# Row normalization on one core: tiles of 16, 12, 12 and 11 rows in turn, with ScalarE summing part of the first tile

## The chip, the core and the metric

The kernel runs on one core of one Trainium2 chip. The metric is device time in microseconds, as a median over several executions. Every execution named here ran at a granted clock of 1.0 and is counted as fast, but for one: the kernel before with six rows reduced once more has an execution of 329.19 us that is classed as slow because it lies over 1.5% above the fastest of its kernel. It is left out of the comparisons. "Span" is the time from the first to the last instruction in the profile; the device time is 1.6 to 2.2 us longer than the span in all runs.

VectorE is written DVE in the profile, ScalarE is ACT, SyncE is SP. ACTq and SPq are the sequencers of ScalarE and SyncE; here their lines show where a DMA is issued.

## The reference

```python
x: float32 [32, 512, 1024]
sums = np.sum(np.abs(x), axis=-1, keepdims=True)
out  = x / (sums + 1e-8)
```

That is 16,384 rows of 1024 floats, or 128 rows of 4 KB on each of the 128 partitions: 67.1 MB read and 67.1 MB written.

## The kernel before

Each tile gives every partition R consecutive rows, so each partition's part of a load or store is one contiguous run of R x 4 KB. All loads are issued by SyncE, all stores by ScalarE. VectorE sums, and VectorE and ScalarE each multiply half of the rows.

```python
    R = 12
    BUFS = 4
    rows = [R] * (per_partition // R)          # ten tiles of 12
    if per_partition % R:
        rows.append(per_partition % R)         # and one of 8
    # ... cut: piece(), which slices x and out by tile ...
    sbuf = ctx.enter_context(tc.tile_pool(name="sbuf", bufs=BUFS))
    stats = ctx.enter_context(tc.tile_pool(name="stats", bufs=4))

    def normalize(x_tile, r0, k, kv):
        s = stats.tile([P, R], FP32)
        nc.vector.tensor_reduce(out=s[:, :k], in_=x_tile[:, r0 : r0 + k, :],
            axis=mybir.AxisListType.X, op=mybir.AluOpType.add,
            apply_absolute_value=True)
        nc.vector.tensor_scalar_add(out=s[:, :k], in0=s[:, :k], scalar1=EPS)
        inv = stats.tile([P, R], FP32)
        nc.vector.reciprocal(out=inv[:, :k], in_=s[:, :k])
        nc.vector.tensor_mul(...)              # rows 0 to kv-1, times inv
        for r in range(kv, k):                 # the other rows, on ScalarE
            nc.scalar.activation(...)          # Copy, scale=inv[:, r]

    with tc.manual_schedule():
        for i, k in enumerate(rows):
            x_tile = sbuf.tile([P, R, d], FP32)
            nc.sync.dma_start(out=x_tile[:, :k, :], in_=piece(x_flat, i))
            normalize(x_tile, 0, k, k // 2)
            nc.scalar.dma_start(out=piece(out_flat, i), in_=x_tile[:, :k, :])
```

With four buffers, loads 0 to 3 are issued at once. Load 4 has to wait until store 0 has landed, load 5 for store 1, and so on. Load 3 is therefore the last load that waits for nothing.

Of the kernel before, what the change touches and what calls it, by code (L numbers as in the profile page):

```python
# [1 line left out]

# [4 lines left out]

FP32 = mybir.dt.float32
EPS = 1e-8


@with_exitstack
def kernel(
    ctx: ExitStack,
    tc: tile.TileContext,
    x: bass.AP,
    out: bass.AP,
):
    nc = tc.nc
    P = nc.NUM_PARTITIONS  # L20

    x_flat = x.flatten_outer_dims()
    out_flat = out.flatten_outer_dims()
    n, d = x_flat.shape


    R = 12
    BUFS = 4
    per_partition = n // P
    assert n % P == 0  # L30
    rows = [R] * (per_partition // R)
    if per_partition % R:
        rows.append(per_partition % R)

    def piece(flat, i):
        a, k = P * sum(rows[:i]), rows[i]
        return flat[a : a + P * k, :].rearrange("(p r) d -> p r d", p=P)

    sbuf = ctx.enter_context(tc.tile_pool(name="sbuf", bufs=BUFS))
    stats = ctx.enter_context(tc.tile_pool(name="stats", bufs=4))  # L40

    def normalize(x_tile, r0, k, kv):

        s = stats.tile([P, R], FP32)
        nc.vector.tensor_reduce(  # L45
            out=s[:, :k],
            in_=x_tile[:, r0 : r0 + k, :],
            axis=mybir.AxisListType.X,
            op=mybir.AluOpType.add,
            apply_absolute_value=True,  # L50
        )
        nc.vector.tensor_scalar_add(out=s[:, :k], in0=s[:, :k], scalar1=EPS)  # L52
        inv = stats.tile([P, R], FP32)
        nc.vector.reciprocal(out=inv[:, :k], in_=s[:, :k])  # L54
        nc.vector.tensor_mul(  # L55
            out=x_tile[:, r0 : r0 + kv, :],
            in0=x_tile[:, r0 : r0 + kv, :],
            in1=inv[:, :kv].unsqueeze(2).to_broadcast([P, kv, d]),
        )
        for r in range(kv, k):  # L60
            row = x_tile[:, r0 + r, :]
            nc.scalar.activation(  # L62
                out=row,
                in_=row,
                func=mybir.ActivationFunctionType.Copy,
                scale=inv[:, r : r + 1],
            )

    with tc.manual_schedule():
        for i, k in enumerate(rows):  # L70
            x_tile = sbuf.tile([P, R, d], FP32)
            nc.sync.dma_start(out=x_tile[:, :k, :], in_=piece(x_flat, i))  # L72
            normalize(x_tile, 0, k, k // 2)
            nc.scalar.dma_start(out=piece(out_flat, i), in_=x_tile[:, :k, :])  # L74


# [1 line left out]
_INS = ['x']  # L78
_OUTS = [((32, 512, 1024), 'float32')]


# [23 lines left out]
```

## Time and profile before

| | before |
|---|---|
| device time, median of 3 | 317.64 us (317.47 to 317.89) |
| span | 315.8 us |
| DVE, ACT busy | 67%, 22% |
| bytes moved | 134.23 MB, 425 GB/s over the span |
| first store issued | 38.45 us |

The page of the profile, cut to the busy rows. Each digit is the busy share of one of 40 slices, in tenths:

```profile
span 315.8 us, 227 instructions
...
## 2 busy tenths in 40 slices
DVE  0069999998499079719944991797099449949300
ACT  0010804308007000700440070007003400701300
...
DMA  8999999999999999999999999999999999999996
```

The DMA row is at 9 but for the first slice and the last, while VectorE has holes. So the engines wait for DMA, and not DMA for them. The next view gives the same for stretches of time. Its columns are start:end, length, busy time and instruction count of DVE, ACT and POOL, granted clock, DMA share, and GB/s. A transfer counts where it starts, so a short stretch can read above or below its share.

```profile
core 0: us, DVE busy (x) ACT busy (x) POOL busy (x), PEclk, DMA share, GB/s
...
83.00:100.00 17.00, 16.63 (x4) 3.28 (x4) 0.00 (x0) 1.00 1.01 439
120.00:160.00 40.00, 30.72 (x8) 11.61 (x12) 0.00 (x0) 1.00 1.00 433
...
200.00:240.00 40.00, 30.88 (x5) 6.34 (x6) 0.00 (x0) 1.00 1.00 433
...
310.00:315.00 5.00, 0.00 (x0) 0.00 (x0) 0.00 (x0) 1.00 0.55 236
315.00:320.00 5.00, 0.00 (x0) 0.00 (x0) 0.00 (x0) 1.00 0.01 2
```

From 83 to 280 us the DMA share is 1.00 to 1.01, at 433 to 439 GB/s. The last row shows that next to nothing moves after 315 us.

The timeline of the first tile (start, length, engine, line, operation, shapes, and in brackets the idle time before it and what ended that):

```profile
18.35 12.95 DVE L45 TENSOR_REDUCE s<-x_tile 128x12 f32<-128x12288 f32 x1 [18.35 <-DMA x_tile<-in_x_dram]
18.40 1.28 ACT L62 ACT_TABLE_LOAD   x1 [18.40 <-DMA x_tile<-in_x_dram]
...
31.81 6.34 ACT L62 ACTIVATE x_tile<-x_tile,inv 128x1024 f32<-128x1024 f32 x6 [12.13 <-DVE inv L54]
31.81 6.56 DVE L55 TENSOR_TENSOR x_tile<-x_tile,inv 128x6144 f32<-128x6144 f32 x1
...
38.45 0.37 ACTq L74 DMA_DIRECT2D out_dram<-x_tile  x1
```

The first tile lands at 18.35 us, is summed for 12.95 us, is multiplied on both engines, and its store is issued at 38.45 us.

A finer reading comes from the trace's records of single DMA packets, which are not a view of the profile. A packet is one partition's run of a tile: 48 KB for 12 rows. A 48 KB packet takes 1.815 us and one of 32 KB takes 1.213 us.

### The profile page before, as it was taken

How to read it: one execution, taken by the hardware profiler on the slowest of the kernel's cores; microseconds unless marked ns; L12 is line 12 of the kernel's file. 1: busy time of each engine (PE TensorE's matmuls, PEld its weight loads, DVE VectorE, ACT ScalarE, POOL GpSimd, SP SyncE). 2: the span in 40 equal slices, each digit the busy share in tenths (PEclk: the TensorE clock that was granted, in tenths of full speed). 3: DMA queues.
4: the chain of work that ended last, by engine and by line, in shares of the span. 5: the costliest groups of instructions: out<-in, count | busy, mean ns of one | idle time of the engine just before them, and what ended most of it. 6: DMA issues, size and time to landing. Idle time of an engine off the chain costs nothing.

```text
span 315.8 us, 227 instructions
## 1 busy us (share of the span) xinstructions
DVE 212.4 (67%) x44; ACT 69.0 (22%) x65; POOL 0.2 (0%) x4
## 2 busy tenths in 40 slices
DVE  0069999998499079719944991797099449949300
ACT  0010804308007000700440070007003400701300
POOL 0000000000000000000000000000000000000000
DMA  8999999999999999999999999999999999999996
GB/s 311 467 417 411 467 367 442 405 454 430 417 448 430 423 461 423 436 442 417 442 442 411 449 436 411 448 436 423 448 430 436 442 413 450 421 448 417 448 403 278
DMA packets 3169, 134.23 MB, mean 425 GB/s; under 512 B 352, under 2 KB 352, under 8 KB 352
## 3 DMA queue, kind: packets, MB, share of 16 engines
q1 hardware_dynamic: 1584, 67.11, 49.8%
q10 hardware_dynamic: 1584, 67.11, 49.1%
q14 instruction: 1, 0.01, 0.0%
HBM read 67.11 MB, written 67.11 MB: 425 GB/s over the span
## 4 chain that ended last, share of the span: by engine, by line
DMA 55%; DVE 25%; another core or an unknown queue 9%; ACT 4%; issue 0%; SPq 0%; DVEq 0%; ACTq 0%
DMA x_tile<-in_x_dram 41%; DVE s L45 19%; DMA out_dram<-x_tile 14%; DVE x_tile L55 6%; ACT x_tile L62 4%; DVE inv L54 0%; DVE s L52 0%; SPq L72 0%; DVEq L54 0%; ACTq L74 0%
## 5 line engine op out<-in xcount | busy, mean ns | idle before, releaser
L45 DVE TENSOR_REDUCE s<-x_tile 128x12 f32<-128x12288 f32 (+1 forms) x11 | 138.2, 12564 | 81.1 <-DMA x_tile<-in_x_dram 81.1
L62 ACT ACTIVATE x_tile<-x_tile,inv 128x1024 f32<-128x1024 f32 x64 | 67.7, 1135 | 207.6 <-DVE inv L54 207.6
L55 DVE TENSOR_TENSOR x_tile<-x_tile,inv 128x6144 f32<-128x6144 f32 (+1 forms) x11 | 70.0, 6364 | 0.4
L62 ACT ACT_TABLE_LOAD x1 | 1.3, 1283 | 18.4 <-DMA x_tile<-in_x_dram 18.4
L54 DVE RECIPROCAL inv<-s 128x12 f32<-128x12 f32 (+1 forms) x11 | 2.5, 226 | 0.9
L52 DVE TENSOR_SCALAR s<-s 128x12 f32<-128x12 f32 (+1 forms) x11 | 1.9, 173 | 0.4
L89 POOL MEMSET const-bfloat16-1.0<- 128x1 bf16 x1 | 0.1, 101 | 0.0
L89 POOL MEMSET const-uint8-127<- 128x1 uint8 x1 | 0.1, 101 | 0.0
L89 POOL MEMSET const-float32-0.0<- 128x1 f32 x1 | 0.1, 98 | 0.2 <-issue 0.2
L89 POOL MEMSET const-float32-1.0<- 128x1 f32 x1 | 0.1, 98 | 0.0
## 6 DMA issues: line engine op xcount, KB each, us to landing
x_tile<-in_x_dram SPq DMA_DIRECT2D x10, 6144.0 KB, 38.5
out_dram<-x_tile ACTq DMA_DIRECT2D x10, 6144.0 KB, 53.5
x_tile<-in_x_dram SPq DMA_DIRECT2D x1, 4096.0 KB, 33.7
out_dram<-x_tile ACTq DMA_DIRECT2D x1, 4096.0 KB, 19.5
```

The costliest lines, as they stand in the source:

```text
L45: nc.vector.tensor_reduce(out=s[:, :k], in_=x_tile[:, r0 : r0 + k, :], axis=mybir.AxisListType.X, op=mybir.AluOpType.add, apply_absolute_v ...
L52: nc.vector.tensor_scalar_add(out=s[:, :k], in0=s[:, :k], scalar1=EPS)
L54: nc.vector.reciprocal(out=inv[:, :k], in_=s[:, :k])
L55: nc.vector.tensor_mul(out=x_tile[:, r0 : r0 + kv, :], in0=x_tile[:, r0 : r0 + kv, :], in1=inv[:, :kv].unsqueeze(2).to_broadcast([P, kv, d]),)
L62: nc.scalar.activation(out=row, in_=row, func=mybir.ActivationFunctionType.Copy, scale=inv[:, r : r + 1],)
L89: nc = _bacc.Bacc("TRN2", target_bir_lowering=False, num_devices=1)
```

## The change

The intent, as the diff reads: give each partition 51 rows of buffers in place of 48, use longer runs in ten tiles rather than eleven, and keep the first store from coming late behind the longer first tile by letting ScalarE sum six of its sixteen rows.

```diff
-    R = 12
-    BUFS = 4
+    R = 16
+    SLOTS = [R, 12, 12, 11]
     # ... cut: rows are taken from SLOTS in turn: 16, 12, 12, 11, 16, 12, 12, 11, 16, 10 ...
-    sbuf = ctx.enter_context(tc.tile_pool(name="sbuf", bufs=BUFS))
+    slots = [
+        ctx.enter_context(tc.tile_pool(name=f"slot{b}", bufs=1))
+        for b in range(len(SLOTS))
+    ]
     stats = ctx.enter_context(tc.tile_pool(name="stats", bufs=4))
+    psum = ctx.enter_context(tc.tile_pool(name="psum", bufs=1, space=bass.MemoryType.PSUM))
+    junk = psum.tile([P, d], FP32)
-    def normalize(x_tile, r0, k, kv):
+    def normalize(x_tile, k, ks, kv):
         nc.vector.tensor_reduce(
-            out=s[:, :k],
-            in_=x_tile[:, r0 : r0 + k, :],
+            out=s[:, :ks],
+            in_=x_tile[:, :ks, :],
             # ... cut ...
+        for r in range(ks, k):
+            nc.scalar.activation(
+                out=junk[:, :],
+                in_=x_tile[:, r, :],
+                func=mybir.ActivationFunctionType.Abs,
+                accum_out=s[:, r : r + 1],
+            )
     # ... cut ...
-            normalize(x_tile, 0, k, k // 2)
+            normalize(x_tile, k, k if i else k * 5 // 8, k // 2)
```

More of the change, by code (lines that the diff above doesn't have):

```diff
@@ L24 @@
     n, d = x_flat.shape
-    R = 12
-    BUFS = 4
-    per_partition = n // P
+    R = 16
+    SLOTS = [R, 12, 12, 11]
     assert n % P == 0
-    rows = [R] * (per_partition // R)
-    if per_partition % R:
-        rows.append(per_partition % R)
+    left = n // P
+    rows = []
+    while left:
+        rows.append(min(left, SLOTS[len(rows) % len(SLOTS)]))
+        left -= rows[-1]
     def piece(flat, i):
@@ L55, in normalize @@
         nc.vector.tensor_mul(
-            out=x_tile[:, r0 : r0 + kv, :],
-            in0=x_tile[:, r0 : r0 + kv, :],
+            out=x_tile[:, :kv, :],
+            in0=x_tile[:, :kv, :],
             in1=inv[:, :kv].unsqueeze(2).to_broadcast([P, kv, d]),
@@ L60, in normalize @@
         for r in range(kv, k):
-            row = x_tile[:, r0 + r, :]
+            row = x_tile[:, r, :]
             nc.scalar.activation(
@@ L70 @@
         for i, k in enumerate(rows):
-            x_tile = sbuf.tile([P, R, d], FP32)
+            x_tile = slots[i % len(SLOTS)].tile([P, SLOTS[i % len(SLOTS)], d], FP32)
             nc.sync.dma_start(out=x_tile[:, :k, :], in_=piece(x_flat, i))
-            normalize(x_tile, 0, k, k // 2)
+            normalize(x_tile, k, k if i else k * 5 // 8, k // 2)
             nc.scalar.dma_start(out=piece(out_flat, i), in_=x_tile[:, :k, :])
```

## The prediction

> **What bounds the kernel now.** The DMA engines, nearly from end to end. The page's DMA row reads 9 in 38 of 40 slices; the windows view gives a DMA share of 1.00 to 1.01 in each stretch from 83 to 280 us, at 433 to 439 GB/s. In the trace's DMA packets all 16 engines have a packet running for about 302 of the 315.8 us. A packet is one partition's 48 KB and takes 1.815 us: 27.1 GB/s an engine, 433 GB/s for sixteen. The Trainium skill, "DMA: Bandwidth & Descriptors", section "Where 436 GB/s comes from", puts the ceiling of the ports at 435.2 GB/s; this trace agrees, at 433. The bytes (134.2 MB) do not change and need about 310 us at that rate. What is left: 1.7 us before the first packet, about 1 us because each engine's first packet takes 2.3 to 3.4 us, about 1 us when the first stores join (one slow load packet per engine after 40 us), and the end (last packet 314.2, span 315.8, time 317.6).
>
> DVE is 67% busy, ACT 22%. DVE waits for loads (81.1 us, by the waits view), which costs nothing while DMA is full. The chain of waits holds compute steps (reduce 19%), but they run beside a full DMA.
>
> **What the change does.**
> - Tiles of 16, 12, 12, 11, 16, 12, 12, 11, 16, 10 rows in place of ten of 12 and one of 8; four buffers still, 51 rows in place of 48.
> - Packets of 64, 48, 44 and 40 KB. From 1.213 us for 32 KB and 1.815 for 48 KB a packet costs some 9 ns plus 0.1505 us a row, so 64 KB should take 2.42 us. Sixteen packets fewer per engine save about 0.15 us.
> - The first load lands later: four rows at 1.21 us, so about 23.2 us in place of 18.35. The first reduce takes ten rows, 10.8 us (12.95/12 a row), while ACT sums six: table load 1.28 us, then six at some 1.1 to 1.4 (estimate from the 1.135 us scale), at most 9.7 us, hidden under the reduce. The multiply of eight rows takes 8.75 us. First store issued near 43.3, in place of 38.45.
> - 16-row tiles later keep DVE 26 us, still under their DMA time of 39 us.
>
> **How much lies on the critical path.** Almost none. I worked the order of packets through with these durations (loads and stores alternating by packet, a load waiting for the store four tiles before). Loads run until about 90 us; store 0 lands near 80, so load 4 is queued before load 3 ends. At no later point are both queues empty. The narrowest place is the end: the last 16-row store is issued near 274 and its predecessor ends near 281; the 10-row store near 291, against 301. A later first store costs nothing: loads fill the time.
>
> **Predicted: 317.4 us, 316.6 to 318.8 in 8 of 10.** Faster by over 2%: 0.01; within 2%: 0.95; slower by over 2%: 0.04.
>
> **What would show it.** Full DMA share from 10 us to 310; 64 KB packets of 2.42 us; first store issued at 43 to 44; the Abs group done before the first reduce; the last load landing near 274; the last packet ending within 1 us of 314.
>
> **What would make it wrong.** A gap in DMA near 80 or 275 to 282 us, if a store is issued later than I reckon. Or 64 KB packets slower than in proportion: their rows start at a power-of-two pitch. The same page ("Latency and other measured facts") measured slower copies from a pitch of 512 KiB up; 64 KiB is well below, and the 8-row tile, at 32 KB, showed none (1.213 us).

## More of the kernel before

Placing each packet after the one that ended as it started sorts them into 16 lanes of 176 packets each, taken here as one lane for each DMA engine (the records do not name the engine). In a lane one packet follows the next without a gap.

Packets that took longer than their size asks for cost 2.19 us per engine in all: 0.96 in the first 5 us, when the first loads start, and 1.16 between 36 and 60 us, when the first store joins.

## The result, and the profile after

| | before | after |
|---|---|---|
| device time, median of 4 | 317.76 us (317.47 to 317.96) | 318.09 us (317.94 to 318.18) |
| ratio after/before | | 1.0011, 95% interval 0.9993 to 1.0028 |
| span | 315.8 us | 315.9 us |
| first store issued | 38.45 us | 42.66 us |
| slow packets, us per engine | 2.19 | 2.06 |
| last data packet ends | 314.2 us | 314.5 us |

A ratio is the mean time of one kernel's runs over that of the other's in the same rounds, so it is not quite the ratio of the medians. The interval includes 1: the two kernels can't be told apart.

The page after, cut to the same rows:

```profile
span 315.9 us, 228 instructions
...
## 2 busy tenths in 40 slices
DVE  0019999999449701999799079807950499999000
ACT  1017730803400800009108000700160002806000
...
DMA  9999999999999999999999999999999999999996
```

The DMA row is the same, while the VectorE row has other holes. The stretches of time, for the changed kernel:

```profile
83.00:100.00 17.00, 8.90 (x1) 0.00 (x0) 0.00 (x0) 1.00 0.99 429
120.00:160.00 40.00, 32.86 (x5) 8.43 (x8) 0.00 (x0) 1.00 0.99 427
...
200.00:240.00 40.00, 21.54 (x5) 9.90 (x10) 0.00 (x0) 1.00 1.00 431
...
310.00:315.00 5.00, 0.00 (x0) 0.00 (x0) 0.00 (x0) 1.00 0.47 205
315.00:320.00 5.00, 0.00 (x0) 0.00 (x0) 0.00 (x0) 1.00 0.01 2
```

The DMA share is 0.99 to 1.00 in the long stretches shown (1.01 in the one from 160 to 200 us), and again nearly nothing moves after 315 us. The first tile:

```profile
0.72 1.28 ACT L61 ACT_TABLE_LOAD   x1 [0.72 <-PEq L106]
...
22.45 10.82 DVE L53 TENSOR_REDUCE s<-x_tile 128x10 f32<-128x10240 f32 x1 [22.45 <-DMA x_tile<-in_x_dram]
22.45 1.03 ACT L61 ACTIVATE junk<-x_tile 128x1024 f32<-128x1024 f32 x1 [20.45 <-DMA x_tile<-in_x_dram]
23.42 0.18 ACT L61 ACTIVATION_READ_ACCUMULATOR junk<-x_tile 128x1 f32 x1
...
29.32 0.18 ACT L61 ACTIVATION_READ_ACCUMULATOR junk<-x_tile 128x1 f32 x1
...
33.88 8.69 DVE L70 TENSOR_TENSOR x_tile<-x_tile,inv 128x8192 f32<-128x8192 f32 x1
33.88 8.42 ACT L77 ACTIVATE x_tile<-x_tile,inv 128x1024 f32<-128x1024 f32 x8 [4.38 <-DVE inv L69]
...
42.66 0.37 ACTq L91 DMA_DIRECT2D out_dram<-x_tile  x1
```

The first tile lands four rows later, at 22.45 us. VectorE sums ten rows in 10.82 us. ScalarE's six sums run beside it and end at 29.5 us, 3.8 us before VectorE's reduce does. The first store is issued at 42.66 us, 4.2 us later than before, and the end of the kernel hardly moves.

Two things about ScalarE's part are seen only here. The groups of instructions (busy us and mean ns after the bar, then idle time):

```profile
L61 ACT ACTIVATE junk<-x_tile 128x1024 f32<-128x1024 f32 x6 | 6.2, 1028 | 20.6 <-DMA x_tile<-in_x_dram 20.4
...
L61 ACT ACT_TABLE_LOAD x1 | 1.3, 1283 | 0.7 <-PEq L106 0.7
L61 ACT ACTIVATION_READ_ACCUMULATOR junk<-x_tile 128x1 f32 x6 | 1.1, 185 | 0.0
```

Each sum is two instructions, the Abs of 1028 ns and a read of the accumulator of 185 ns, and they start 1.18 us apart. The table load of 1283 ns ran at 0.72 us, while ScalarE had nothing to do, and not after the landing as I had assumed. The Trainium skill, "ScalarE: Activation LUTs", section "What ACT_TABLE_LOAD costs", gives about 1283 ns for that load; this trace has the same.

### The profile page after: what moved, and what is told of

It is laid out like the page before. It is cut to its first block, busy times and chain, and to the rows that moved or that the text cites. A ratio compares the mean times of both kernels' runs of the same rounds, so it can differ in the third digit from the quotient of the medians.

```text
span 315.9 us, 228 instructions
## 1 busy us (share of the span) xinstructions
DVE 204.2 (65%) x40; ACT 76.8 (24%) x78; POOL 0.2 (0%) x4
## 4 chain that ended last, share of the span: by engine, by line
DMA 37%; another core or an unknown queue 29%; DVE 26%; SPq 0%; issue 0%; DVEq 0%; ACTq 0%
DMA x_tile<-in_x_dram 21%; DVE s L53 16%; DMA out_dram<-x_tile 16%; DVE x_tile L70 9%; SPq L87 0%; DVE inv L69 0%; DVE s L67 0%; DVEq L69 0%; DVEq L67 0%; ACTq L91 0%
## 5 line engine op out<-in xcount | busy, mean ns | idle before, releaser
L53 DVE TENSOR_REDUCE s<-x_tile 128x12 f32<-128x12288 f32 (+3 forms) x10 | 131.6, 13164 | 86.5 <-DMA x_tile<-in_x_dram 86.5
L77 ACT ACTIVATE x_tile<-x_tile,inv 128x1024 f32<-128x1024 f32 x65 | 68.6, 1135 | 194.0 <-DVE inv L69 194.0
L70 DVE TENSOR_TENSOR x_tile<-x_tile,inv 128x6144 f32<-128x6144 f32 (+2 forms) x10 | 68.8, 6878 | 0.3
L61 ACT ACTIVATE junk<-x_tile 128x1024 f32<-128x1024 f32 x6 | 6.2, 1028 | 20.6 <-DMA x_tile<-in_x_dram 20.4
L69 DVE RECIPROCAL inv<-s 128x12 f32<-128x12 f32 (+3 forms) x10 | 2.3, 234 | 0.8
L67 DVE TENSOR_SCALAR s<-s 128x12 f32<-128x12 f32 (+3 forms) x10 | 1.7, 174 | 0.4
L61 ACT ACT_TABLE_LOAD x1 | 1.3, 1283 | 0.7 <-PEq L106 0.7
L61 ACT ACTIVATION_READ_ACCUMULATOR junk<-x_tile 128x1 f32 x6 | 1.1, 185 | 0.0
## 6 DMA issues: line engine op xcount, KB each, us to landing
out_dram<-x_tile ACTq DMA_DIRECT2D x1, 5120.0 KB, 22.4
```

Of the source, the lines that this page charges most:

```text
L53: nc.vector.tensor_reduce(out=s[:, :ks], in_=x_tile[:, :ks, :], axis=mybir.AxisListType.X, op=mybir.AluOpType.add, apply_absolute_value=True,)
L61: nc.scalar.activation(out=junk[:, :], in_=x_tile[:, r, :], func=mybir.ActivationFunctionType.Abs, accum_out=s[:, r : r + 1],)
L70: nc.vector.tensor_mul(out=x_tile[:, :kv, :], in0=x_tile[:, :kv, :], in1=inv[:, :kv].unsqueeze(2).to_broadcast([P, kv, d]),)
L77: nc.scalar.activation(out=row, in_=row, func=mybir.ActivationFunctionType.Copy, scale=inv[:, r : r + 1],)
```

## The experiments

**Theory going in:** the 16 DMA engines are full, so the time is the start, plus the bytes at their rate, plus the end. When the first store comes does not matter as long as loads last. **Rival:** the two halves of the change cancel; the bigger tiles make the first store later and cost time, and ScalarE's sums win it back.

### Both halves alone, and no compute at all

**The changed kernel without ScalarE's sums.**

```diff
-            normalize(x_tile, k, k if i else k * 5 // 8, k // 2)
+            normalize(x_tile, k, k, k // 2)
```

> The changed kernel without ScalarE's sums in the first tile: the first reduce takes 17.2 us in place of 10.8, so the first store is issued near 49 us in place of 42.7. Theory (the 16 DMA engines are full from 4 us on, so the time is start + bytes at their rate + end, and the moment of the first store does not matter): 318.1 us, within 0.5 us of the changed kernel. Rival (the two halves of the change cancel: bigger tiles cost what the later first store loses, and ScalarE's sums win it back): some 6 us slower, near 324.

Measured: 324.55 us median of 6, ranging from 322.38 to 326.01, ratio to before 1.0214 (1.0177 to 1.0252): slower beyond the noise, though whether by over 2% is unclear. **My theory missed; the rival's number came in.** The timeline of its first tile shows that the edit did what was meant:

```profile
22.61 17.22 DVE L53 TENSOR_REDUCE s<-x_tile 128x16 f32<-128x16384 f32 x1 [22.61 <-DMA x_tile<-in_x_dram]
...
40.36 8.69 DVE L70 TENSOR_TENSOR x_tile<-x_tile,inv 128x8192 f32<-128x8192 f32 x1
...
49.13 0.38 ACTq L91 DMA_DIRECT2D out_dram<-x_tile  x1
```

Its page:

```profile
span 321.2 us, 216 instructions
...
DMA  9999999999997999999999999999999999999993
```

Still nearly all nines, so the 6 us are no gap that this row could show. Its last stretches:

```profile
310.00:315.00 5.00, 0.00 (x0) 0.00 (x0) 0.00 (x0) 1.00 0.89 385
315.00:320.00 5.00, 0.00 (x0) 0.00 (x0) 0.00 (x0) 1.00 0.30 131
```

In the kernel before, data after 315 us came to 2 GB/s over five microseconds. Here 131 GB/s still move there: some engines are late. The completion records say how many. The first engine to finish its last store reported at 314.1 us, close to the 313.2 us of before. Six engines were done by 314.6 us, and the other ten followed between 315.8 and 320.1 us; in before the last one reported at 314.7 us. Slow packets cost 5.31 us per engine on average, in place of 2.06 in the changed kernel. The records of three lanes, two of this run and one of the changed kernel (L is a load, S a store, then rows, start + length in us; * marks a packet slower than its size asks for):

```
no ScalarE sums, a lane:   L11:55.7+1.67 S16:57.4+3.06* L11:60.4+1.67 S16:62.1+3.31* L11:65.4+1.67 S16:67.1+3.54*
no ScalarE sums, another:  L11:57.3+1.67 S16:59.0+2.42 L11:61.4+2.19* S16:63.6+2.42 L11:66.0+2.16* S16:68.1+2.43
changed kernel, a lane:    L11:61.5+1.67 S16:63.2+2.42 L11:65.6+1.67 S16:67.3+2.42 L11:69.7+1.67 S16:71.3+2.42
```

Loads and stores alternate packet by packet, as the Trainium skill, "DMA: Bandwidth & Descriptors", section "Queues, rings and completion order", says of an engine with work from two queues. In the slow run the engines fell into two groups, one starting a store while the other loads, and packets in both are slow while store 0 goes out. Sixteen more slow ones, one per engine on average, come at 95 to 96 us, when load 4 joins the running stores (2.5 to 4.6 us in place of 2.42). In the changed kernel all 16 engines load and store in step.

**The kernel before with ScalarE's sums, and nothing else.**

```diff
+        for r in range(ks, k):
+            nc.scalar.activation(out=junk[:, :], in_=x_tile[:, r, :],
+                func=mybir.ActivationFunctionType.Abs, accum_out=s[:, r : r + 1])
-            normalize(x_tile, 0, k, k // 2)
+            normalize(x_tile, 0, k, k // 2, k if i else 7)
```

(The reduce takes the first `ks` rows, as in the change; junk is the same PSUM tile.)

> The kernel before with ScalarE summing five of the first tile's twelve rows and nothing else changed: the first reduce takes 7.6 us in place of 12.95, so the first store is issued near 33 us in place of 38.4. Theory: 317.8 us, within 0.5 us of before. Rival (halves cancel): some 5 us faster, near 312.5.

Measured: 317.72 us, ratio 1.0001 (0.9989 to 1.0013), with the first store issued at 33.28 us. Here my theory held and the rival missed by 5 us: an earlier first store gains nothing.

**The kernel before with no compute** (the line that calls `normalize` is taken out; a wrong result).

> The kernel before with all compute taken out, so that it only loads and stores (wrong result on purpose): a floor. First store issued near 18.5 us. Theory: DMA was full already, so 317 to 318 us, at most 1 us under before. Rival (compute is on the path, as the chain of waits with 25% DVE may suggest): clearly faster, 300 us or less if a quarter of the chain went.

Measured: 317.45 us, ratio 0.9993 (0.9981 to 1.0005). Its page:

```profile
span 315.4 us, 80 instructions
...
DMA  8999999999999999999999999999999999999996
```

This is a floor for this pattern of loads and stores, and both kernels already stand within 0.7 us of it. Compute that is only made quicker cannot win anything here. Yet the first experiment shows that compute can still lose.

### The slow packets when stores start

**The kernel before with the first load split over two queues.**

```diff
+            if i == 0:
+                h = k // 2
+                nc.sync.dma_start(out=x_tile[:, :h, :], in_=src[:, :h, :])
+                nc.scalar.dma_start(out=x_tile[:, h:k, :], in_=src[:, h:, :])
```

> The kernel before with the first load in two halves, rows 0 to 5 from SyncE's queue and rows 6 to 11 from ScalarE's. About 40 us from the start of before, one load packet per engine takes 2.6 to 3.2 us in place of 1.815, when the first stores join: 1.1 us per engine in all. Theory A (that is the price of the first use of the second queue): the slow packets near 40 us go, and the time falls by about 1 us, to 316.8. Theory B (it is the price of the first data going out of SBUF): the slow packets stay and the time is within 0.4 us of before.

Measured: 317.69 us, ratio 1.0002 (0.9990 to 1.0014). Between 36 and 60 us 22 packets are still slow, for 1.08 us per engine. So it is not the first use of the second queue that costs this; here it comes when the first stores join running loads. That it is the stores as such is not shown, and two later runs (first store at 66 and 84 us) speak against it: their first stores, with no load running, take at most 2.47 us in place of 2.42, and 32 slow packets, loads and stores, come instead when load 4 joins the stores, for 2.3 us per engine. Nothing is won.

### How late may the first store be?

**The changed kernel, with the first tile's 16 rows reduced twice, and three times** (`for _ in range(times)` around the first tile's reduce, times = 2 and 3; the result is the same).

> The changed kernel with the first tile's reduce over all 16 rows run twice on VectorE (the same result): first store issued near 66 us. The four buffers hold 51 rows, which loads alone fill by 64.4 us (at 1.213 us a row). Theory (only a gap in DMA costs): DMA idles for about 3.4 us from 64.4, so 321.5 us (320.5 to 322.5). Rival 1 (the first store's delay is passed on): about 23 us slower, 341. Rival 2 (later slack takes it all up): 318.1.

> The same with the reduce run three times: first store issued near 84 us. Theory: a DMA gap of about 20.6 us from 64.4, so 338.7 us (337 to 340.5), every further microsecond of delay now passed on one for one (17.2 more than the run with two reduces). Rival 1 (delay passed on from the first microsecond): near 359. Rival 2 (slack takes it up): 318.

Measured: 322.11 us (321.72 to 322.69) and 339.0 us (338.94 to 339.26), with the first store at 66.3 and 83.6 us. Both numbers came in. The last load that waits for nothing landed at 64.9 and 65.0 us, and from then until the store there is nothing to move. For the second, in stretches:

```profile
50.00:60.00 10.00, 9.97 (x2) 0.00 (x0) 0.00 (x0) 1.00 1.00 433
60.00:65.00 5.00, 5.00 (x1) 0.00 (x0) 0.00 (x0) 1.00 0.67 288
65.00:70.00 5.00, 5.00 (x1) 0.00 (x0) 0.00 (x0) 1.00 0.00 0
70.00:80.00 10.00, 9.90 (x4) 5.14 (x5) 0.00 (x0) 1.00 0.00 0
80.00:84.00 4.00, 4.00 (x2) 3.28 (x4) 0.00 (x0) 1.00 0.00 0
84.00:90.00 6.00, 6.00 (x1) 0.00 (x0) 0.00 (x0) 1.00 1.22 524
```

From 65 to 84 us DMA moves nothing. From that point every microsecond of delay is passed on. But 322.11 us, with a real gap of some 3 us and with these slow packets, is *less* than the 324.55 us of the run with its store at 49 us and no gap.

### Less buffer, smaller tiles

**The kernel before with BUFS = 3.**

> The kernel before with three buffers of 12 rows in place of four. If DMA need only be kept from running empty, 36 rows nearly suffice: worked through packet by packet, one gap of about 1 us near 304 us, at the end, when the last store is issued just after the one before has gone: 318.8 us (317.8 to 320). Rival (buffer capacity is what the time hangs on, so that 51 rows against 48 should have helped): several us slower, over 322.

Measured: 318.72 us (318.50 to 319.13), ratio 1.0040. The short gap is where it was reckoned:

```profile
302.00:304.00 2.00, 2.00 (x1) 2.00 (x3) 0.00 (x0) 1.00 0.91 393
304.00:306.00 2.00, 0.50 (x1) 0.28 (x1) 0.00 (x0) 1.00 0.61 262
306.00:308.00 2.00, 0.00 (x0) 0.00 (x0) 0.00 (x0) 1.00 1.16 492
```

The last store is issued at 304.58 us, just as its predecessor runs out. Losing a quarter of the buffers costs 1 us, by a gap that the kernel before does not have, so 51 rows in place of 48 had hardly anything to gain.

**The kernel before with R = 4 and BUFS = 12.**

> The kernel before with 4 rows a tile and 12 buffers, the same 48 rows in all. From the packets' durations (1.213, 1.815, 2.418 us for 32, 48, 64 KB) each packet costs about 9 ns besides its bytes; this kernel has 512 packets per engine in place of 176 and needs 3.0 us more by that: 320.8 us (320 to 322.5). Rival (smaller tiles start stores sooner and end sooner, so finer is better): under 316.

Measured: 318.39 us, ratio 1.0025 (1.0010 to 1.0040). It is slower, as expected, but by 0.7 us and not 3. A 16 KB packet does take 0.611 us, as the 9 ns a packet would have it. But the records of neighbouring packets overlap a little, here by 1.76 us per engine and in before by 0.50, and slow packets cost less here, 1.36 us per engine against 2.19. Taken off the 3.0 us, that leaves 3.0 - 1.26 - 0.83 = 0.9 us, near the 0.7 measured. So the 9 ns that I read off the durations overstate what a packet costs in time.

### Lateness, tile sizes, or something else?

The first experiment needed a new theory. Theory A: lateness of the first store costs about its own length. Theory B: it takes unequal packets (64 KB stores against 44 KB loads) and a chance split of the engines, or a load queue that has run dry.

**The changed kernel with ScalarE summing three rows** (13 in place of `k * 5 // 8`).

> The changed kernel with ScalarE summing three of the first sixteen rows in place of six: first reduce over 13 rows, first store issued near 46 us (42.7 in the changed kernel, 49.1 with no ScalarE sums, which came out 6 us slower). Theory A (a later first store costs about as much as it is late): near 321.5. Theory B (the run with no ScalarE sums was slow because its first store split the 16 DMA engines into two groups half a load-store cycle apart, and 64 KB stores against 44 KB loads then ran slow until that store had gone, and because the load queue ran dry near 85 us): here the store still joins while 48 KB loads run and lands near 84 us, before the last of load 3, so 318.1 us (317.5 to 319) unless the engines split again.

Measured: 318.9 us (318.46 to 319.72), ratio 1.0041. That is theory B's range, and no 3.4 us for 3.4 us of lateness.

**The changed kernel with no ScalarE sums and six rows reduced once more first.**

```diff
+        if again:
+            nc.vector.tensor_reduce(out=s[:, :again], in_=x_tile[:, :again, :], ...)
-            normalize(x_tile, k, k if i else k * 5 // 8, k // 2)
+            normalize(x_tile, k, k, k // 2, 0 if i else 6)
```

> The changed kernel with no ScalarE sums and six rows reduced once more first: first store issued near 55.6 us, while all engines load the 44 KB packets of tile 3. Theory A (lateness costs): near 330, or at least above 325. Theory B (gaps, the price of a queue starting again, and a chance split): loads run dry near 71 us while stores go on, so no gap, one more start of a queue of about 1 to 2 us: 319 to 320.5 us, faster than with the store at 49; above 322 only if the engines split here too.

Measured: 318.74 us median of 4 (317.56 to 321.6), ratio 1.0047 (0.9984 to 1.0111). The first store is 7 us *later* than in the run that took 324.55 us, and the time is 6 us shorter. Theory A falls. The median is just under theory B's range. Its price for a queue that starts again did not show: the loads ran dry at 75.4 us and began again at 85, with one slow packet. One of the four executions, not the profiled one, still took 321.6 us, near the loss of the slow run; in the profiled one 15 engines were done by 313.7 us and one at 316.0.

**The kernel before with six rows reduced once more first** (the same edit; all its packets are 48 KB, but for the last tile).

> The kernel before with six rows of the first tile reduced once more first: first store issued near 44.9 us in place of 38.4, the same lateness of 6.4 us that cost 6 us in the unequal tiles, here with loads and stores of one size, 48 KB. Theory A (lateness costs in any kernel): near 323. Theory B (it took unequal packets, or a dry load queue; here store 0 lands near 77 us and load 3 near 83): 317.7 us, within 0.6 us of before.

Measured: 323.31 us median of three executions (322.23 to 325.39), ratio 1.0187 (1.0137 to 1.0237): slower beyond the noise, by over 2% or not unclear. With the execution at 329.19 us and the same clock, the median of four is 324.35, the figure that the next expectation uses. **Theory B missed; theory A's number came in:** the loss is there with equal packets too. Only its clause about a dry load queue is left: load 3 landed at 76.7 us and store 0 at 78.5 us, where I had reckoned with 83 and 77. The end shows late engines again:

```profile
310.00:315.00 5.00, 0.00 (x0) 0.00 (x0) 0.00 (x0) 1.00 0.68 295
315.00:320.00 5.00, 0.00 (x0) 0.00 (x0) 0.00 (x0) 1.00 0.12 52
```

The first engine finished its last store at 313.5 us, the last at 320.2 us; eleven were done by 314.7. Averaged over the engines slow packets cost only 3.10 us here, 0.9 more than in before, so the loss lies with a few engines. Right after the first store joined, 14 of the 16 lanes ran in step at full speed. Two lanes, about 1 us behind the others, had slow load packets (2.1 to 2.5 us in place of 1.815). Such packets came back later, up to 276 us.

**The same with all twelve rows reduced once more first** (12 in place of 6). This tested theory C, formed from the table below without its row: the loss comes when store 0 lands within about 2 us of the end of load 3.

> The kernel before with all twelve rows of the first tile reduced once more first: first store issued near 51.4 us, 13 us later than in before and 6.5 later than in the run that came out 6.6 us slower (324.35). The size theory fell there, as all its packets are 48 KB. Theory A (lateness of the first store costs about its own length): near 330. Theory C (the loss comes when store 0 lands within a couple of microseconds of the end of load 3, the last load that needs no wait: margins of -0.2 and -1.8 us in the two slow runs, and of 10 us and more, either way, in fast ones): here load 3 should end near 67 us and store 0 land near 77, a margin of -10 us with no gap in DMA: 318 to 319.5 us, faster than the run with the earlier store.

Measured: 317.98 us median of 5 (317.43 to 318.33), ratio 1.0016 (1.0002 to 1.0029). The first store is 6.6 us later than in the run before, and 5.3 us are back (the two ran on different chips, each beside the kernel before). The margin measured is -7.3 us, not the -10 expected. The expectation also overlooked a fast run, the one with three sums, at a margin of only +4.2. The end is again that of the kernel before:

```profile
310.00:315.00 5.00, 0.00 (x0) 0.00 (x0) 0.00 (x0) 1.00 0.50 216
315.00:320.00 5.00, 0.00 (x0) 0.00 (x0) 0.00 (x0) 1.00 0.00 2
```

The table puts the runs side by side. Landings come from the completion records in the trace of each profiled execution (those of the two slower kernels, which this section calls the slow runs, took 323.12 and 323.31 us, both at clock 1.0): the time at which the last of the 16 engines reported. The margin is the landing of load 3 less that of store 0; a negative one means that the load queue stood empty before load 4 could be issued.

```
                                     first    load 3  store 0           first..last engine     time, us
                                     store    lands   lands    margin   done with last store   (median)
before, ScalarE sums 5 rows          33.28     89.0    68.2    +20.8    313.3 .. 315.0         317.72
before                               38.45     83.2    73.6     +9.6    313.2 .. 314.7         317.76
changed kernel                       42.66     91.1    80.4    +10.7    313.1 .. 314.8         318.09
changed, ScalarE sums 3 rows         46.11     87.8    83.6     +4.2    313.1 .. 315.4         318.90
changed, no ScalarE sums             49.13     89.8    90.0     -0.2    314.1 .. 320.1         324.55
before, 6 rows reduced again         45.20     76.7    78.5     -1.8    313.5 .. 320.2         323.31
before, 12 rows reduced again        51.78     70.6    77.9     -7.3    313.1 .. 314.9         317.98
changed, no sums, 6 rows again       56.09     75.4    85.1     -9.7    313.0 .. 316.0         318.74
changed, 16 rows reduced twice       66.32     64.9    87.1    -22.2    317.7 .. 319.0         322.11
changed, 16 rows reduced 3 times     83.64     65.0   104.4    -39.4    335.1 .. 336.3         339.00
```

What follows: the median stays within about 1.2 us of before where the margin is 4 us or more away from zero and DMA has no gap, and is about 6 us longer in the two runs where it is near zero (the size varies: 322.38 to 326.01 us in the one). It rises again when DMA has a real gap (the last two rows). Theory C made its prediction before the last run and kept it. That tested only its fast side: no new run was sent into the bad place. It is a rule over ten runs and no mechanism. In both slow runs slow packets came well before load 3 had ended, so an empty load queue alone is not their cause.

A rival fits as well, and these runs can't separate it: what matters may be where the first store joins. Each tile is eight packets per engine. In the two slow runs each lane had started 25 or 26 load packets before its first store packet, so that the store joined one or two packets into load 3; in the table's other runs without a gap it was 19 to 24, or 29 and 30. As load 3 then has about as many packets left as the store has, a margin near zero follows from this. The two slow runs were on different chips, so it is not one chip. Why two lanes or one group of lanes slow down, when in other runs lanes out of step do not, **stays open**.

The loss itself is shown: it is engines that finish late (ten of 16 in one slow run, five in the other) while the rest are done at about 314 us. They can't catch up, because every load and store gives each engine the same share. Each of the 16 lanes of before holds 176 packets, 16 for each of the 11 tiles. The Trainium skill, "DMA: Bandwidth & Descriptors", section "The descriptor swizzle", describes this fixed map, eight partitions to an engine; these counts agree with it.

## Why the prediction was right, and where it was not

- **What bounds the kernel: right.** The copy with no compute takes 317.45 us. (The prediction's 302 us understate how full DMA is: they come out if only moments with exactly 16 packets are counted. With those in which neighbouring records overlap, so that 17 or more run, it is 310 us.) The ceiling of 435.2 GB/s that I took from the skill fits the long stretches: 433 GB/s over 120 to 160 us in before, 427 in after.
- **The time: right.** 317.4 us predicted, 318.09 measured, inside 316.6 to 318.8. The 0.15 us from fewer packets can't be seen; the 0.3 us by which the change is slower is inside the noise.
- **The steps of the first tile: right, with two sizes off.** First load 22.45 us (23.2 predicted), first reduce 10.82 (10.8), multiply 8.69 (8.75), first store 42.66 (43.3). The landing was mis-sized by 0.75 us: I scaled the 18.35 us of before, whose engines reported over 1.0 us (17.3 to 18.3), and in after they report within 0.3 us (22.1 to 22.4). The table load was off the path altogether.
- **The queues: right for this kernel.** Store 0 lands at 80.4 us (80 predicted), load 3 ends at 91.1 (90), the last load lands at 275.1 (274), the last packet ends at 314.5 (314). 64 KB packets take 2.418 us (2.42); the feared power-of-two pitch cost nothing, at 64 KB.
- **The step that failed: "A later first store costs nothing: loads fill the time."** It holds at 42.66 us and fails at 49.13 us, where loads fill the time too: 324.55 us. I treated 16 engines as one. A packet order worked out for one average engine shows a gap only if all are idle; it can't show that some fall behind. I did not ask what happens when store 0 lands as load 3 ends. That the changed kernel's own store stays clear of this, by 10.7 us, was in the working; that it had to was not, so in this the right number owes something to luck.
- **What ScalarE's sums are worth.** By the prediction, nothing. By the runs, about 6 us in the changed kernel (324.55 against 318.09), because without them the first store falls into what the table shows as the bad place (delaying it further, with no ScalarE sums, also brings the time back: 318.74), and nothing in the kernel before (317.72 against 317.76). The bigger tiles and the sums together come out even. So the rival, that two halves cancel, was right about the changed kernel's numbers, but "later costs more" is not the reason: later still was faster.

No version beat both kernels: the fastest that compute anything, the kernel before with a split first load (317.69 us) and with ScalarE's sums (317.72 us), are the same as before, and the copy is at 317.45 us.

## What to carry to other kernels

When DMA is full from end to end, compare with a copy that has the same loads and stores before touching the compute: here it showed 0.3 us to win. Then look at when the first buffer's store lands against when the last free-running load ends, and keep the two well apart, by ten microseconds in both kernels here (a rule of thumb from these runs, with its cause open); a half of a change that wins nothing by itself may be what keeps them apart. If the time jumps with the DMA row still at nines, compare when the first and the last DMA engine finish.

## What the Trainium skill lacked or had wrong

- "DMA: Bandwidth & Descriptors": apart from a remark on engines 7 and 15, which it ties to DMA issued from GpSimd, nothing says that some of the 16 engines can fall behind the others in a kernel of plain, equal loads and stores issued from SyncE and ScalarE. Here this cost 6 us: first engine done at 314.1 us, last at 320.1, with 64 KB store packets of up to 3.5 us in place of 2.42.
- The same page: nothing on what it costs when one queue joins another that is running. In before about one load packet per engine takes 2.6 to 3.2 us in place of 1.815, 1.16 us per engine between 36 and 60 us; using the second queue earlier for a load does not take it away. Where loads joined running stores it was 2.3 us per engine in two runs, and nothing in another.
- The same page, section "Where 436 GB/s comes from", says that for transfers between HBM and SBUF the HBM side binds, at about 358 GB/s a core (though its own table has 425 for a large load on one core, and "HBM Reference" names about 425 for a core streaming alone). Here loads and stores together run at 433 GB/s over stretches of 40 us, so for this one core it was the 435 that fitted, and not the 358.
- "ScalarE: Activation LUTs" names an accumulator output of ACTIVATE, but gives neither the second instruction that reads the accumulator nor its time ("VectorE: DVE Perf Modes" says of such an op only that it is two instructions). The runs show 185 ns for it, and sums of 1024 columns starting 1.18 us apart.
